# Splitting a block's weights into high and low parts 1024 columns at a time

## The chip, the core and the metric

The kernel runs on one core of one Trainium2 chip. Its time is the device time of one execution in microseconds; lower is better. The engines of a core work side by side: TensorE (PE, matrix products and transposes), VectorE (DVE), ScalarE (ACT), GpSimd (POOL), and SyncE (SP), which here only issues DMA transfers.

## The reference

One decoder layer on 512 tokens of width 1024, in float32. A normalized input is projected by one matrix of 6936 columns; the columns feed two token mixers in parallel. Mixer A is sparse attention with eight heads of 64 in two groups (compressed keys through a small two-layer network per 32 tokens, selected blocks, a window). Mixer B is retention with four heads, in chunks of 128. Gates merge both, and one output projection and a second norm follow.

```python
h = rms_norm(x, norm_pre)
proj = h @ w_in
(q_n, k_c, v_c, k_s, v_s, k_w, v_w, g_n, z_n,
 q_r, k_r, v_r, z_r, m_a, m_b) = jnp.split(proj, split_points(), axis=-1)
...
y_a = (o_a * jax.nn.silu(z_n)) @ w_nsa_o
y_b = (o_b * jax.nn.silu(z_r)) @ w_ret_o
merged = jax.nn.sigmoid(m_a) * y_a + jax.nn.sigmoid(m_b) * y_b
x = x + rms_norm(merged @ w_out, norm_post)
```

## The kernel before

**Two parts for every operand.** Products keep near float32 precision by splitting each operand into a high part (the value rounded to fp32r, a float32 format that TensorE takes) and a low part (value minus high part, also fp32r). A product is then three matmuls: high by high, high by low, low by high. Activations are split where they arise; weights are split as they stream in.

**The weight stream.** All weights lie in one DRAM array in the order of use, in loads of 128 partitions by 1024 columns (560 for block C): two *halves* of 512 (280) columns, each the rows k of one step of 128 of a product's inner dimension. `load_next` (line 323) loads them into a ring of four `raw` tiles. `splitter` takes half after half: `cp_any` rounds it into a `whi` tile (line 197 on ScalarE, or line 205 on VectorE where that engine would be done sooner), and `split_lo` subtracts into a `wlo` tile (line 209 on VectorE, through `sub_split` and `tt`). There are nine `whi` and nine `wlo` tiles of 512 columns (`NW`). A half may be split once the half nine places before it has been used up by its last matmul. Block C has buffers of its own (`WC`).

**Blocks.** The program on TensorE goes block by block: A (512 columns, all four token tiles at once, k by k), C (280 columns), Q, two hidden blocks of the compression network (`hidden`: each half is used by four matmuls of 256 columns and is then free), then by `PLAN` the blocks Z, MA, ZR, QK, VR, ZR, QK, VR, MB, NO, RO, MA, MB, NO, RO, and two output blocks. Most blocks have eight halves and run in four passes (`nat`, `tra`): each pass is one tile of the output and uses all eight halves with three matmuls each, so the halves become free one by one during the last pass. Transposes are matmuls by an identity (line 234); all other matmuls are at line 230. Attention, retention and the tails that evict results are written as further coroutines.

**The order of the work.** The class `Order` runs these coroutines when the program is built. It keeps a clock for TensorE and one for each other engine, advanced by a cost formula per instruction, and issues the coroutine of the lowest priority number that is ready by its clock; `main` with the blocks has the last priority, so that whatever else is ready goes ahead of it. What comes out is a fixed list of instructions for each engine: at run time each engine works through its list in order and waits for what its next instruction needs. A split has priority 0 if its half is at most two ahead (`SOON`) of the one that `main` wants, and 4, after all attention work, otherwise (`rank`). `split_lo` holds back while VectorE's planned backlog exceeds `SLACK`, 700 ns, unless its rank is 0.

Of the kernel before, what the change touches and what calls it, by code (L numbers as in the profile page):

```python
# [11 lines left out]
FR = mybir.dt.float32r  # L12
# [6 lines left out]
P = 128  # L19
SEQ, D = 512, 1024  # L20
NT = SEQ // P
KD = D // P
# [2 lines left out]

C_Q, C_A, C_C, C_Z = 0, 512, 1024, 1304
C_QR, C_KR, C_VR, C_ZR, C_MA, C_MB = 1816, 2328, 2840, 3864, 4888, 5912
NR, NW = 4, 9
PLAN = (("Z", 0), ("MA", 0), ("ZR", 0), ("QK", 0), ("VR", 0), ("ZR", 1), ("QK", 1), ("VR", 1),
        ("MB", 0), ("NO", 0), ("RO", 0), ("MA", 1), ("MB", 1), ("NO", 1), ("RO", 1))  # L30
MAIN = 9
# [114 lines left out]
def block_kernel(ctx: ExitStack, tc, x, xT, g_pre, ws, small, w2s, norm_post, rope_r, dmask, out):  # L146
# [6 lines left out]
    wp = ctx.enter_context(tc.tile_pool(name="wts", bufs=1))  # L153
# [9 lines left out]
    def at(kb, n, dt=FT):  # L163
        o = int(kb * 256)
        return (arena_r if dt == FR else arena_f)[:, o:o + n]
# [6 lines left out]
    od = Order()  # L172
# [27 lines left out]
    def cp_any(o, i, r=0.0):  # L200

        cd = copy_ns(o, i)
        if od.begin("act", r) + act_ns(o, i) <= od.begin("dve", r, near(i)) + cd + DVE_BIAS:
            return act(o, i, r=r)
        V.tensor_copy(o, i)
        return od.op("dve", cd, r, near(i))
# [35 lines left out]
    def sub_split(lo, src, hi, r, e="dve"):  # L242
        return tt(lo, src, f(hi), OP.subtract, r, e)
# [59 lines left out]
        off += P * sum(pieces)  # L303

    raws, parts, done = [], [], []
    WC = [tuple(at(44, 4480, FR)[:, (2 * p + i) * 280:(2 * p + i + 1) * 280] for i in range(2)) for p in range(KD)]

    def in_ring(p):

        return min(p, KD) + max(p - 2 * KD, 0)  # L310
    hook = {}

    def queue(i, j):

        return S if i + j == 0 else DMA

    def load_next():
        i = len(raws)
        if i < len(loads):
            raw = rp.tile([P, 1024], FT, name="raw", tag="raw", bufs=NR)  # L320
            o, c, r = loads[i][0], 0, parts[2 * (i - NR) + 1][2] if i >= NR else 0.0
            for j, n in enumerate(loads[i][1]):
                queue(i, j).dma_start(raw[:, c:c + n], ws[o:o + P * n].rearrange("(p n) -> p n", p=P))
                e = od.dma(P * n * 4, r)
                o, c = o + P * n, c + n
            raws.append((raw, e))
            for fn in hook.get(i, ()):
                fn()
# [5 lines left out]
    nxt = [0]  # L334

    def splitter():
        for i, (_, pieces) in enumerate(loads):
            n = sum(pieces)
            for k in range(2):
                p = 2 * i + k  # L340
                own = KD <= p < 2 * KD
                yield lambda: own or in_ring(p) < in_ring(len(done)) + NW
                while len(raws) <= i:
                    yield lambda: len(raws) > i or len(raws) < NR or len(parts) > 2 * (len(raws) - NR) + 1
                    if len(raws) <= i:
                        load_next()
                r = max(raws[i][1], done[-1] if done and not own else 0.0)
                yield r, "act"
                m = n // 2
                src = raws[i][0][:, k * m:(k + 1) * m]  # L350
                if own:
                    hi, lo = WC[p - KD]
                else:
                    hi = wp.tile([P, 512], FR, name="whi", tag="whi", bufs=NW)
                    lo = wp.tile([P, 512], FR, name="wlo", tag="wlo", bufs=NW)
                vh, vl = hi[:, :m], lo[:, :m]
                e = cp_any(vh, src, r)
                od.spawn(split_lo(p, hi, lo, src, vh, vl, e), rank(p))
                nxt[0] = p + 1
                yield  # L360

    def split_lo(p, hi, lo, src, vh, vl, r):
        yield lambda: rank(p)() == 0 or od.eng["dve"] <= od.now + SLACK
        yield r
        r = sub_split(vl, src, vh, r)
        yield lambda: len(parts) == p
        parts.append((hi, lo, r))
        if p % 2 and len(raws) <= p // 2 + NR:
            load_next()

    used, wanted = [0], [0]
# [1 line left out]
    def rank(p):  # L373

        return lambda: 0 if p <= wanted[0] + SOON else 4
# [911 lines left out]
    od.spawn(h_split(), 0)  # L1287
    od.spawn(norms(), 1)
    od.spawn(splitter(), lambda: rank(nxt[0])())
    od.spawn(edges(), 1)  # L1290
    od.spawn(main(), MAIN)
# [101 lines left out]
```

## Time and profile before

| what | us |
|---|---|
| median of three runs | 531.09 |
| lowest and highest run | 531.02, 531.74 |
| profiled execution, first to last instruction | 529.4 |
| TensorE busy | 519.1 |
| VectorE busy | 390.4 |
| ScalarE busy | 253.4 |

The profiled execution has 7318 instructions; its own time is known by its span alone, which begins at the first and ends at the last instruction. The granted clock of TensorE is at full speed in all 40 slices of the page:

```profile
PEclk9999999999999999999999999999999999999999
```

In the lists below a name such as `bank` or `wlo` is that of a tile; `arena_f` and `arena_r` are two large tiles in which most intermediate results have a place; `nat` are four work tiles. A time "x7" in a row covers seven instructions in a row. Lengths of instructions that follow each other overlap a little, so that the distance from start to start, and not the length, is what an engine needs for one.

### The profile page before, as it was taken

Reading aid. Unit: us, or ns where it says so; the run is one execution under the profiler, and the core shown is the slowest. Engines: PE = TensorE matmul, PEld = TensorE weight load, DVE = VectorE, ACT = ScalarE, POOL = GpSimd, SP = SyncE. Lnnn points to the kernel's source line nnn. Section 1 sums busy time; section 2 is a strip of 40 time slices with the busy share of each in tenths; the row PEclk is TensorE's granted clock in tenths of the full one; section 3 lists DMA queues with packets and bytes.
Section 4 is the critical chain, followed back from the end, with each engine's and each line's share of the span. In section 5 each row is a group of like instructions: output and inputs, shape, how many; then the busy total and the mean of one; then the engine's idle time right before and its main releaser. Section 6 shows DMA issues by size and latency. Waiting matters only on the chain.

```text
span 529.4 us, 7318 instructions
## 1 busy us (share of the span) xinstructions
PE 519.1 (98%) x2636; PEld 437.3 (83%) x2636; DVE 390.4 (74%) x925; ACT 253.4 (48%) x551; POOL 12.6 (2%) x32
## 2 busy tenths in 40 slices
PE   8998999999999999999999999999999999999995
PEld 7896888888888888888888888888888888888885
DVE  6799799989989899998767896777737235345533
ACT  6764588537356494565636253525304224123411
POOL 1000000000000000000010000000000000000000
PEclk9999999999999999999999999999999999999999
DMA  8931127401313013150412342131814043304022
GB/s 327 381 121 54 46 75 251 153 1 42 119 40 109 13 40 120 40 194 5 143 38 80 99 132 67 41 120 40 316 43 158 17 142 121 119 1 158 1 98 101
DMA packets 18131, 55.18 MB, mean 104 GB/s; under 512 B 2096, under 2 KB 3120, under 8 KB 18096
## 3 DMA queue, kind: packets, MB, share of 16 engines
q1 hardware_dynamic: 17808, 54.46, 30.2%
q8 instruction: 20, 0.33, 0.3%
q10 hardware_dynamic: 288, 0.27, 0.2%
q14 instruction: 15, 0.12, 0.1%
HBM read 52.63 MB, written 2.10 MB: 103 GB/s over the span
## 4 chain that ended last, share of the span: by engine, by line
PE 89%; DVE 7%; issue 2%; DMA 1%; ACT 0%; POOLq 0%; DVEq 0%; POOL 0%; ACTq 0%
PE bank L230 83%; PE bank L234 6%; DVE arena_f L209 2%; DVE wlo L209 2%; DVE arena_r L209 1%; DMA raw<-in_stream_dram 1%; DVE arena_f L519 1%; DVE nat L209 0%; DVE arena_f L218 0%; DVE arena_f L798 0%; ACT nat L197 0%; DVE arena_f L222 0%; ACT whi L197 0%; POOLq L1389 0%; POOL rr L209 0%
## 5 line engine op out<-in xcount | busy, mean ns | idle before, releaser
L197 ACT ACTIVATE whi<-raw 128x512 fp32r<-128x512 f32 x150 | 89.8, 627 | 51.2 <-PE bank L230 43.6
L209 DVE TENSOR_TENSOR wlo<-raw,whi 128x512 fp32r<-128x512 f32 x160 | 103.2, 686 | 7.2 <-ACT whi L197 6.5
L230 PE MATMUL bank<-whi,hTh 128*128 128x512 f32 x256 | 98.9, 401 | 0.8 <-ACT whi L197 0.8
L230 PE MATMUL bank<-wlo,hTh 128*128 128x512 f32 x256 | 96.3, 391 | 0.0
L230 PE MATMUL bank<-whi,hTl 128*128 128x512 f32 x256 | 96.2, 391 | 0.0
L230 PE MATMUL bank<-arena_r 128*128 128x256 f32 (+2 forms) x328 | 69.7, 335 | 0.0
L197 ACT ACTIVATE arena_r<-bank 128x512 fp32r<-128x512 f32 (+2 forms) x80 | 44.6, 571 | 47.9 <-PE bank L234 47.7
L230 PE MATMUL bank<-hTh,whi 128*128 128x512 f32 x160 | 63.2, 395 | 0.0
L230 PE MATMUL bank<-hTh,wlo 128*128 128x512 f32 x160 | 62.5, 391 | 0.0
L230 PE MATMUL bank<-hTl,whi 128*128 128x512 f32 x160 | 62.4, 390 | 0.0
L230 PE MATMUL bank<-arena_r,whi 128*128 128x512 f32 x192 | 59.2, 389 | 0.0
L230 PEld LDWEIGHTS bank<-whi,hTl 128*128 128x128 f32 x256 | 48.0, 188 | 10.5
L230 PEld LDWEIGHTS bank<-arena_r 128*128 128x128 f32 x328 | 51.1, 190 | 6.1 <-DVE stat L798 0.2
L230 PEld LDWEIGHTS bank<-whi,hTh 128*128 128x128 f32 x256 | 48.1, 188 | 9.5 <-ACT whi L197 1.0
L230 PEld LDWEIGHTS bank<-wlo,hTh 128*128 128x128 f32 x256 | 48.2, 188 | 9.0 <-DVE wlo L209 0.4
L209 DVE TENSOR_TENSOR arena_r<-bank,arena_r 128x512 fp32r<-128x512 f32 (+2 forms) x72 | 46.5, 656 | 7.4 <-ACT arena_r L197 6.8
L230 PE MATMUL bank<-whi,arena_r 128*128 128x512 f32 (+1 forms) x176 | 48.8, 351 | 0.0
L230 PEld LDWEIGHTS bank<-arena_r,whi 128*128 128x128 f32 x192 | 36.0, 188 | 7.6 <-DVE sg L222 0.2
L234 PE MATMUL bank<-ident,arena_f 128*128 128x128 f32 (+1 forms) x260 | 37.1, 274 | 1.6 <-DVE arena_f L519 1.0
L234 PEld LDWEIGHTS bank<-ident,arena_f 128*128 128x128 f32 (+1 forms) x260 | 30.4, 138 | 8.4 <-DVE arena_f L519 1.5
L230 PE MATMUL bank<-arena_r,wlo 128*128 128x512 f32 x96 | 37.4, 389 | 0.0
L197 ACT ACTIVATE arena_f<-arena_f,stat 128x512 f32<-128x512 f32 (+3 forms) x64 | 35.3, 555 | 3.5 <-DVE stat L798 3.4
(117 smaller groups left out, 670.7 us busy)
## 6 DMA issues: line engine op xcount, KB each, us to landing
raw<-in_stream_dram SPq DMA_DIRECT2D x79, 512.0 KB, 3.9
arena_f<-in_x_dram SPq DMA_DIRECT2D x8, 512.0 KB, 7.1
arena_f<-in_xT_dram SPq DMA_DIRECT2D x8, 256.0 KB, 5.8
arena_f<-in_rope_r_dram SPq DMA_DIRECT2D x8, 256.0 KB, 2.6
out_dram<-arena_f SPq DMA_DIRECT2D x6, 256.0 KB, 2.0
raw<-in_stream_dram SPq DMA_DIRECT2D x4, 280.0 KB, 7.1
arena_f<-in_norm_post_dram SPq DMA_DIRECT2D x1, 512.0 KB, 7.8
out_dram<-arena_f SPq DMA_DIRECT2D x2, 192.0 KB, 1.9
```

The costliest lines, as they stand in the source:

```text
L197: S.activation(o, i, func, **kw)
L209: (V if e == "dve" else G).tensor_tensor(o, a, b, op=op)
L230: T.matmul(ps, a, b, start=start, stop=stop)
L234: T.transpose(ps, a, idn)
L519: V.tensor_copy(kd.rearrange("p (a r c) -> p a r c", a=n, r=2), kn[:, a:b].rearrange("p (a c) -> p a c", c=64).unsqueeze(2).broadcast_to([ ...
```

## The change

From load 4 on (`WHOLE`), that is for all blocks but A, both halves of a load are rounded by one instruction over 1024 columns (560 for C) and subtracted by another. For A's four loads the two halves are split one after the other as before. The `whi` and `wlo` tiles are 1024 columns wide and there are four of each (`NW // 2` with `NW` = 8), so that a pair of halves shares one buffer and the buffer is free when both halves are used up. Both halves of a pair get the rank of the first. The stream, the loads and all matmuls and transposes stay the same in number and size; 160 subtractions of 512 columns become 76 of 1024 and 8 of 512, and 8 of 280 become 4 of 560.

```diff
-NR, NW = 4, 9
+NR, NW, WHOLE = 4, 8, 4
...
-    WC = [tuple(at(44, 4480, FR)[:, (2 * p + i) * 280:(2 * p + i + 1) * 280] for i in range(2)) for p in range(KD)]
+    WC = [tuple(at(44, 4480, FR)[:, (2 * q + i) * 560:(2 * q + i + 1) * 560] for i in range(2)) for q in range(KD // 2)]
...
     def splitter():
         for i, (_, pieces) in enumerate(loads):
             n = sum(pieces)
-            for k in range(2):
-                p = 2 * i + k
-                own = KD <= p < 2 * KD
-                yield lambda: own or in_ring(p) < in_ring(len(done)) + NW
-                while len(raws) <= i:
-                    yield lambda: len(raws) > i or len(raws) < NR or len(parts) > 2 * (len(raws) - NR) + 1
-                    if len(raws) <= i:
-                        load_next()
-                r = max(raws[i][1], done[-1] if done and not own else 0.0)
+            own = KD <= 2 * i < 2 * KD
+            yield lambda: own or in_ring(2 * i) + 2 <= in_ring(len(done)) + NW
+            while len(raws) <= i:
+                yield lambda: len(raws) > i or len(raws) < NR or len(parts) > 2 * (len(raws) - NR) + 1
+                if len(raws) <= i:
+                    load_next()
+            r = max(raws[i][1], done[-1] if done and not own else 0.0)
+            if own:
+                hi, lo = WC[i - KD // 2]
+            else:
+                hi = wp.tile([P, 1024], FR, name="whi", tag="whi", bufs=NW // 2)
+                lo = wp.tile([P, 1024], FR, name="wlo", tag="wlo", bufs=NW // 2)
+            whole = i >= WHOLE
+            for k in range(1 if whole else 2):
                 yield r, "act"
-                m = n // 2
-                src = raws[i][0][:, k * m:(k + 1) * m]
-                if own:
-                    hi, lo = WC[p - KD]
-                else:
-                    hi = wp.tile([P, 512], FR, name="whi", tag="whi", bufs=NW)
-                    lo = wp.tile([P, 512], FR, name="wlo", tag="wlo", bufs=NW)
-                vh, vl = hi[:, :m], lo[:, :m]
+                c = slice(0, n) if whole else slice(k * (n // 2), (k + 1) * (n // 2))
+                src, vh, vl = raws[i][0][:, c], hi[:, c], lo[:, c]
                 e = cp_any(vh, src, r)
-                od.spawn(split_lo(p, hi, lo, src, vh, vl, e), rank(p))
-                nxt[0] = p + 1
+                od.spawn(split_lo(2 * i + k, n // 2, 2 if whole else 1, src, vh, vl, e), rank(2 * i + k))
+                nxt[0] = 2 * i + k + (2 if whole else 1)
                 yield
 
-    def split_lo(p, hi, lo, src, vh, vl, r):
+    def split_lo(p, m, n, src, vh, vl, r):
...
-        parts.append((hi, lo, r))
-        if p % 2 and len(raws) <= p // 2 + NR:
+        for k in range(n):
+            parts.append((vh[:, k * m:(k + 1) * m], vl[:, k * m:(k + 1) * m], r))
+        if len(parts) % 2 == 0 and len(raws) <= p // 2 + NR:
             load_next()
```

Since costs and buffers enter the plan, the lists of TensorE, VectorE, ScalarE and SyncE come out in another order; GpSimd's list stays the same. Three places follow.

*VectorE, tails of blocks A and C.* `nat_100`, `nat_102` hold key tiles, `arena_f<-bank,cst` of 64 partitions adds the position bias to transposed keys and frees a bank, `arena_r<-arena_f,arena_r` of 128x16x64 splits the result. Before:

```order
L209 TENSOR_TENSOR arena_f<-bank_85,cst 64x2x8x16 x4
L209 TENSOR_TENSOR arena_r<-bank_86,arena_r 128x2x128
L209 TENSOR_TENSOR wlo<-raw,whi 128x512
L209 TENSOR_TENSOR arena_f<-nat_102,cst 128x32
L209 TENSOR_TENSOR arena_f<-nat_102,cst 128x2x8 x2
L209 TENSOR_TENSOR nat_102<-arena_f 128x2x16
L209 TENSOR_TENSOR wlo<-raw,whi 128x512
L209 TENSOR_TENSOR arena_f<-bank_86,cst 64x2x8x16 x4
L209 TENSOR_TENSOR wlo<-raw,whi 128x512 x2
```

With the change:

```order
L209 TENSOR_TENSOR arena_r<-bank_85,arena_r 128x2x128
L209 TENSOR_TENSOR wlo<-raw,whi 128x1024
L209 TENSOR_TENSOR arena_r<-bank_86,arena_r 128x2x128
L209 TENSOR_TENSOR arena_f<-nat_102,cst 128x32
L209 TENSOR_TENSOR arena_f<-nat_102,cst 128x2x8 x2
L209 TENSOR_TENSOR nat_102<-arena_f 128x2x16
L209 TENSOR_TENSOR arena_f<-bank_85,cst 64x2x8x16 x4
L209 TENSOR_TENSOR arena_f<-bank_86,cst 64x2x8x16 x4
L209 TENSOR_TENSOR arena_r<-arena_f,arena_r 128x16x64 x2
```

The single subtractions around the position-bias adds have become one pair ahead of them, and the adds of the last two tiles stand together.

*VectorE and TensorE, from the hidden blocks to Z.* VectorE's list with the change, from the last pair of the hidden blocks (the first row) over the gelu of the first hidden block (the rows of 128x128) to Z's four pairs:

```order
L209 TENSOR_TENSOR wlo<-raw,whi 128x1024
L209 TENSOR_TENSOR arena_r<-bank_85,arena_r 128x512
L226 RECIPROCAL stat<-stat 128x1
L218 TENSOR_SCALAR arena_f<-arena_f,stat,gate 128x512
L209 TENSOR_TENSOR wlo<-raw,whi 128x1024 x2
L209 TENSOR_TENSOR arena_f<-bank_86,arena_f 128x128
L209 TENSOR_TENSOR arena_f<-arena_f 128x128
L218 TENSOR_SCALAR arena_f<-arena_f 128x128
L209 TENSOR_TENSOR arena_f<-arena_f 128x128
L209 TENSOR_TENSOR wlo<-raw,whi 128x1024 x2
```

TensorE's list at the start of Z before (`bank_81<-hTh,whi` is Z's first matmul of a half, the others are attention):

```order
L230 MATMUL bank_81<-hTh,whi 128x512
L230 MATMUL bank_81<-hTl,whi 128x512
L230 MATMUL bank_81<-hTh,wlo 128x512
L230 MATMUL bank_83<-arena_r 128x512 x2
L230 MATMUL bank_81<-hTh,whi 128x512
L230 MATMUL bank_81<-hTl,whi 128x512
L230 MATMUL bank_81<-hTh,wlo 128x512
L234 MATMUL bank_86<-ident,arena_f 128x128 x4
L234 MATMUL bank_85<-ident,arena_f 128x128 x4
```

With the change the first seven halves of Z, 21 matmuls, follow each other without other work between them.

*VectorE, from RO 1 to the first output block.* `sg` rows are the tails of RO's last two tiles, `arena_r<-sg` the split of the merged result. Before:

```order
L209 TENSOR_TENSOR wlo<-raw,whi 128x512
L209 TENSOR_TENSOR arena_r<-sg_106,arena_r 128x512
L205 CAST whi<-raw 128x512
L209 TENSOR_TENSOR wlo<-raw,whi 128x512 x5
L222 SCALAR_TENSOR_TENSOR arena_f<-arena_f,bank_82 128x512
L209 TENSOR_TENSOR sg_107<-sg_107,arena_f 128x512
L209 TENSOR_TENSOR wlo<-raw,whi 128x512 x2
L209 TENSOR_TENSOR arena_r<-sg_107,arena_r 128x512
```

With the change:

```order
L209 TENSOR_TENSOR wlo<-raw,whi 128x1024
L209 TENSOR_TENSOR arena_r<-sg_106,arena_r 128x512
L209 TENSOR_TENSOR wlo<-raw,whi 128x1024
L222 SCALAR_TENSOR_TENSOR arena_f<-arena_f,bank_82 128x512
L209 TENSOR_TENSOR sg_107<-sg_107,arena_f 128x512
L209 TENSOR_TENSOR wlo<-raw,whi 128x1024 x2
L209 TENSOR_TENSOR arena_r<-sg_107,arena_r 128x512
```

Six of the eight halves stood ahead of the last tile's tail, now two pairs, four halves.

## The prediction

> **What bounds the kernel now.** I read the page's busy table first, then the engines by stretches, the chain that ended last in order of time, and the single instructions where that chain leaves TensorE.
>
> ```profile
> PE 519.1 (98%) x2636; PEld 437.3 (83%) x2636; DVE 390.4 (74%) x925; ACT 253.4 (48%) x551; POOL 12.6 (2%) x32
> ```
>
> TensorE is busy for 98% of the span, so 80 instructions fewer on VectorE and 75 fewer on ScalarE can shorten only the stretches where TensorE waits. The same engines by stretch (columns: length, then PE, PEld, DVE, ACT, POOL busy with counts, clock, DMA):
>
> ```profile
> 27.30:52.30 25.00, 23.21 (x154) 20.05 (x153) 23.85 (x78) 13.33 (x36) 0.94 (x4) 1.00 0.24 81
> 68.00:85.60 17.60, 17.27 (x110) 14.70 (x108) 16.75 (x44) 15.24 (x32) 0.00 (x0) 1.00 0.44 133
> 92.00:250.00 158.00, 158.00 (x823) 132.97 (x822) 145.21 (x395) 91.47 (x230) 0.00 (x0) 1.00 0.22 74
> 250.00:365.00 115.00, 115.00 (x604) 98.05 (x603) 87.68 (x195) 49.82 (x96) 5.96 (x8) 1.00 0.26 83
> ```
>
> Of these only the first two leave TensorE idle, 25.00 - 23.21 = 1.8 us and 0.3 us; there VectorE is busy 95% of the time. From 92 to 250 us it is 92% busy as well, but TensorE never runs dry. The chain says the same (start, length, what):
>
> ```profile
> 27.27 0.70 ACT nat L197
> ...
> 52.24 0.44 PE bank L234 x2
> ...
> 67.97 0.70 ACT nat L197
> ...
> 85.58 1.23 PE bank L230 x7
> ...
> 365.89 152.55 PE bank L230 x676
> ```
>
> VectorE leads from 27.3 to 52.2 us (tails of blocks A and C) and from 68.0 to 85.6 us (end of Q, the two hidden blocks). Behind that TensorE leads: 152.55/676 = 0.226 us for a matmul, so 0.68 us for the three of one half.
>
> **The change, part by part.** *What one merged instruction costs.* Groups, then single instructions on VectorE:
>
> ```profile
> L209 DVE TENSOR_TENSOR wlo<-raw,whi 128x512 fp32r<-128x512 f32 x160 | 103.2, 686 | 7.2 <-ACT whi L197 6.5
> L197 ACT ACTIVATE arena_f<-arena_f 128x1024 f32<-128x1024 f32 x4 | 4.2, 1062 | 1.8 <-DMA arena_f<-in_x_dram 1.3 <-DVE arena_r L209 0.6
> L197 ACT ACTIVATE whi<-raw 128x512 fp32r<-128x512 f32 x150 | 89.8, 627 | 51.2 <-PE bank L230 43.6 <-DMA raw<-in_stream_dram 5.3 <-ACT whi L197 0.4
> ```
> ```profile
> 52.10 1.22 DVE L209 TENSOR_TENSOR arena_r<-arena_f,arena_r 128x1024 fp32r<-128x1024 f32 x1
> 53.24 0.29 DVE L519 COPY arena_f<-nat 128x256 f32<-128x256 f32 x1
> 372.75 2.49 DVE L209 TENSOR_TENSOR wlo<-raw,whi 128x512 fp32r<-128x512 f32 x4
> ```
>
> The kernel already has a 1024-wide subtraction of the same kind: 1.22 us alone, and the next instruction starts 53.24 - 52.10 = 1.14 us later. Four 512-wide ones in a row take 2.49 us, which is (2.49 - 0.69)/3 = 0.60 us from one to the next. A pair so costs 1.14 in place of 1.20 us: 0.06 us saved, 76 times, 4.6 us of VectorE's 390. On ScalarE the 1024-wide form takes 1.06 us at most (that row also sums its squares) against two of 0.63 us, which overlap a little. All of it lies under TensorE's work except in the two stretches.
>
> [...]
>
> *The ring.* Nine halves become four pairs. A block of eight halves fills them, so nothing of the next block can be split until the last pass over the current one has used up a whole pair. A pair is free 6 halves before it is needed (it was 8 with nine singles), 6 x 0.68 = 4.1 us (5.4). The way from a free buffer to ready weights is 1.06 + 1.22 us and two handovers of up to 0.2 us, 2.7 us, against 0.63 + 0.69 + 0.4 = 1.7 us. The spare time falls from 3.7 to 1.4 us at every block boundary. How far VectorE is behind at such a place shows here, at the boundary before the first output block:
>
> ```profile
> 480.23 0.68 DVE L222 SCALAR_TENSOR_TENSOR arena_f<-arena_f,bank 128x512 f32<-128x512 f32 x1
> ...
> 481.55 1.28 DVE L209 TENSOR_TENSOR wlo<-raw,whi 128x512 fp32r<-128x512 f32 x2
> ```
> ```profile
> 482.35 0.39 PE L230 MATMUL bank<-wlo,arena_r 128*128 128x512 f32 x1
> ```
>
> The first row opens the tail of the last tile of RO 1. The new order puts the pairs for k = 4, 5 and 6, 7 behind the first two instructions of that tail (last place above), so the first of them starts at 481.55 and is ready at 481.55 + 1.14 = 482.69 us; TensorE wants its low part at 482.35 us. Wait: 0.3 us. The other late boundaries have one tail less in the way, or read the low part last: 0 us, bounds 0 to 0.3 us for this term.
>
> *First stretch.* The adds of the position bias have this row:
>
> ```profile
> L209 DVE TENSOR_TENSOR arena_f<-bank,cst 64x256 f32<-64x256 f32 x14 | 8.6, 614 | 0.2
> ```
>
> The new order has two pairs where VectorE had six single subtractions; the second half of the next tiles' keys moves behind them (first place above). VectorE has 6 x 0.60 - 2 x 1.14 = 1.3 us less to do there. But TensorE's transposes are moved too: a transpose needs a bank that four such adds (2.4 us) empty, and laying the rows' lengths end to end in the new order I find TensorE waiting for them four times, 0.3, 0.6, 0.3 and 0.6 us (an estimate), 1.8 us in all against 1.8 us idle now. I take -0.1 us, which is the two merged pairs; bounds -1.3 (all of it reaches TensorE) and +0.5 us (one more of those waits).
>
> *Hidden blocks.* The hidden blocks start at the first row, and block Z starts at the last; between them eight transposes, after four matmuls of the first hidden block:
>
> ```profile
> 75.35 0.28 PE L230 MATMUL bank<-whi,arena_r 128*128 128x256 f32 x1
> ...
> 75.81 1.03 PE L234 MATMUL bank<-ident,arena_f 128*128 128x128 f32 x8
> 76.60 0.36 PE L230 MATMUL bank<-whi,arena_r 128*128 128x256 f32 x1
> ...
> 90.56 0.40 PE L230 MATMUL bank<-hTh,whi 128*128 128x512 f32 x1
> ```
>
> From first to last stand 15.2 us, and by these pitches about 12.9 us of TensorE work (64 matmuls of 256 columns at (75.81 - 75.35)/4 = 0.115 us, 24 transposes at (76.60 - 75.81)/8 = 0.10 us, ten matmuls of 512 columns at 0.226 us, six small ones, an estimate of 0.8 us): 2.3 us of waiting, because TensorE uses a half in four matmuls, 0.46 us, and VectorE makes one in 0.60 us. Eight pairs take 9.1 instead of 9.6 us, and the new order puts more attention work between them. I take -0.5 us, bounds -1.0 and 0.
>
> *Start of Z.* The rows that the new order strings together:
>
> ```profile
> 84.18 0.16 DVE L226 RECIPROCAL stat<-stat 128x1 f32<-128x1 f32 x1
> ...
> 84.84 1.29 DVE L209 TENSOR_TENSOR wlo<-raw,whi 128x512 fp32r<-128x512 f32 x2
> 86.04 0.29 DVE L209 TENSOR_TENSOR arena_f<-bank,arena_f 128x128 f32<-128x128 f32 x1
> ...
> 87.16 1.28 DVE L209 TENSOR_TENSOR wlo<-raw,whi 128x512 fp32r<-128x512 f32 x2
> ```
> ```profile
> 91.25 0.62 PE L230 MATMUL bank<-arena_r 128*128 128x512 f32 x2
> 91.70 0.39 PE L230 MATMUL bank<-hTh,whi 128*128 128x512 f32 x1
> ```
>
> From the last hidden pair to Z's third pair VectorE has: one 512-wide subtraction 0.60, reciprocal and scaling 84.84 - 84.18 = 0.66, two pairs 2.28, the four gelu steps 87.16 - 86.04 = 1.12, a pair 1.14: 5.8 us. TensorE, over the same way, has eight hidden matmuls 0.9, two attention matmuls 91.70 - 91.25 = 0.45, two transposes 0.2, and 14 matmuls of Z without any filler between them 3.2: 4.8 us. It waits 1.0 us if both start level; before, Z's first halves had attention work between them (91.25 is the first) and waited for nothing. Bounds 0 and 1.0; VectorE is the later engine there, so I take 0.7 us.
>
> *Loads.* Each stream load still brings both halves, and the next is issued when its pair is split, as before behind the second half. Their cover is that a raw tile is loaded a block ahead; without it a landing of 3.9 us would show.
>
> ```profile
> raw<-in_stream_dram SPq DMA_DIRECT2D x79, 512.0 KB, 3.9
> ```
>
> *Sum.* -0.1 - 0.5 + 0.7 + 0.3 = +0.4 us on the profiled span of 529.4 us, 529.8 us. The median of the runs, 531.09 us, is 1.7 us above that span (what lies around the instructions); I keep this, and forecast 531.5 us, no change that can be told. About 0.2% (1.06 us) is what a measurement here can tell from none.
>
> **The rivals.** *Faster*: the stretches led by VectorE shorten by all that it saves, and the fillers still suffice at Z: -1.3 - 0.5 = -1.8 us, 529.3 us. For it speaks that VectorE is on the chain for 42 us; against it that the order of TensorE is fixed when the program is written, by costs that let VectorE be earlier than it is, and the waits come from that, not from the subtractions.
>
> *Slower*: the spare 1.4 us at block boundaries is too little while VectorE is 92% busy. From 92 to 365 us there are eight boundaries. Where a pair finds another pair and one other instruction ahead of it, 1.14 + 0.69 = 1.83 us, TensorE waits 1.83 - 1.4 = 0.43 us; eight times is 3.4 us, 534.5 us. It decides once VectorE is more than 1.4 us behind at a boundary and no attention or retention matmul stands in the gap. For it: the row of 92 to 250 us. Against: TensorE has over 800 instructions there, many of them attention work that fills gaps.
>
> *No saving at all*: the 1024-wide forms cost twice the 512-wide ones. The row of 1.22 us speaks against it; it would move the forecast by +0.6 us, to 532.1 us, still no change.
>
> **How the numbers follow.** No change 0.42 (with the last rival in it), own range 530.2 to 532.1 us; faster 0.27; slower 0.31, since of the bounds -1.3, -1.0, 0, 0 and +0.5, 0, +1.0, +0.3 with up to 3.4 us at the boundaries the losses reach farther. The whole range is 529.4 to 534.2 us: it goes to the faster rival's time and nearly to the slower one's, and leaves out about one in five.
>
> **What would show it.** Merged subtractions 1.14 us apart, whi in at most 1.06 us. TensorE idle from 27 to 52 us near 1.8 us again: first stretch right; under 0.8 us: the faster rival. From the end of Q to Z less waiting than 2.3 us, and a wait for wlo of up to 1 us in Z's first tile. A row of TensorE waiting for wlo at 482 us, by 0.3 us. Idle TensorE between 92 and 365 us, where it has none, is the slower rival. I am wrong if the waits between blocks there add up to over 1 us, or if TensorE's idle time in the first stretch halves.

## The result, and the profile after

| kernel | median, us | lowest and highest | profiled span |
|---|---|---|---|
| before, six runs beside after | 531.41 | 531.02, 533.40 | 529.4 |
| after, six runs | 535.17 | 534.22, 536.92 | 532.5 |

The ratio is 1.0062 with a 95% interval of 1.0043 to 1.0081: slower by 3.3 us (the medians stand 3.8 us apart, the profiled spans 3.1 us). The forecast was 531.5 us, no change, range 529.4 to 534.2 us. The runs of most kernels here fall on two levels 1.5 to 2 us apart, so that ratios compare whole sets of runs; in the profiles of e2, e7, e9, e12, e14, e15 and e17 TensorE gets its full clock at 9.5 to 10.8 us, not at 4.5 to 6.0 us as in the others, and loses some 2 us more in the first 27 us, ahead of all that is changed.

What the merged instructions themselves cost came out as forecast. The busy row of the page of after, and two groups with shapes kept apart:

```profile
PE 521.2 (98%) x2636; PEld 436.3 (82%) x2636; DVE 383.5 (72%) x840; ACT 247.1 (46%) x476; POOL 15.4 (3%) x32
...
L209 DVE TENSOR_TENSOR wlo<-raw,whi 128x1024 fp32r<-128x1024 f32 x76 | 91.4, 1219 | 8.1 <-ACT whi L197 7.4
L197 ACT ACTIVATE whi<-raw 128x1024 fp32r<-128x1024 f32 x73 | 77.0, 1058 | 43.1 <-PE bank L230 37.2 <-DMA raw<-in_stream_dram 3.6 <-ACT whi L197 1.1
```

VectorE has 6.9 us less to do (390.4 before; 4.6 us were forecast) and ScalarE 6.3 us less; TensorE's matmuls and transposes are the same 2636, and yet the span is 3.1 us longer.

To see where, I add up from the trace, for each matmul and transpose, by how much the start of the next one comes later than is usual after one of its kind. These are sums over all 2636, in us of waiting by stretch:

| stretch, us | before | after | e1 | e3 | e5 | e6 | e9 | e10 | e13 | e14 |
|---|---|---|---|---|---|---|---|---|---|---|
| 27 to 53, A and C | 3.5 | 4.8 | 3.6 | 3.4 | 3.5 | 4.7 | 4.2 | 4.6 | 3.0 | 2.9 |
| 68 to 100, hidden, Z | 2.4 | 2.4 | 2.1 | 2.7 | 1.2 | 2.4 | 3.7 | 5.1 | 5.6 | 7.2 |
| 100 to 250 | 1.6 | 3.1 | 3.4 | 4.6 | 2.6 | 1.2 | 4.2 | 4.4 | 2.8 | 4.3 |
| 250 to 300 | 0.7 | 1.4 | 0.6 | 1.4 | 6.0 | 4.4 | 1.8 | 1.7 | 1.0 | 1.9 |
| 300 to 365 | 0.8 | 0.9 | 0.9 | 0.9 | 0.8 | 0.8 | 1.6 | 0.8 | 1.3 | 0.8 |

(e1 to e14 are the experiments below; matmuls at a lower clock count as waiting here. What counts as usual is a choice: another one shifts a row as a whole, and differences between kernels by 0.4 us at most.) After loses 1.2 us in the tails of A and C and 2.2 us from 100 to 300 us; the rest nearly cancels.

**Block boundaries.** The waits of weight loads (PEld, TensorE's load of one operand of a matmul) for low parts from 92 to 365 us, first of before, then of after (us in total, times, longest):

```profile
PEld bank L230 <- DVE wlo L209: 0.4, 1, 0.4
```
```profile
PEld bank L230 <- DVE wlo L209: 3.3, 10, 0.5
```

Ten short waits for low parts where there was one. One of the ten lies in a hidden block, at 92.4 us; the other nine lie in the first pass of a block, each at the first half of a pair. They aren't all of the 2.2 us: from 100 to 300 us weight loads wait 4.6 us in after and 0.7 us in before, and 2.9 and 0.4 us of that is for low parts, the rest for other results of VectorE. (A weight load waits longer than the matmuls lose: 0.46 us against 0.2 us in the example.) The example, VectorE's list and then TensorE's:

```profile
263.86 1.02 DVE L209 TENSOR_TENSOR arena_r<-arena_f,arena_r 128x512 fp32r<-128x512 f32 x2
264.79 2.35 DVE L209 TENSOR_TENSOR wlo<-raw,whi 128x1024 fp32r<-128x1024 f32 x2
```
```profile
265.64 0.40 PE L230 MATMUL bank<-whi,hTh 128*128 128x512 f32 x1
266.06 0.50 PE L230 MATMUL bank<-wlo,hTh 128*128 128x512 f32 x1
```

The high part is there at 265.64 us. Its low part is ready when the first of the two pairs ends, at 264.79 + 1.22 = 266.01 us, and the matmul starts at 266.06 us instead of 265.64 + 0.23 = 265.87 us. Nothing else stood in that gap, and two splits of another result stood ahead of the pair.

**The norm row.** ScalarE, then TensorE:

```profile
49.86 1.06 ACT L197 ACTIVATE arena_r<-arena_f 128x1024 fp32r<-128x1024 f32 x1 [5.84 <-DVE arena_f L209]
51.11 1.06 ACT L197 ACTIVATE arena_r<-arena_f 128x1024 fp32r<-128x1024 f32 x1 [0.20 <-DVE arena_f L209]
52.08 0.58 ACT L197 ACTIVATE rsrow<-bank 128x512 f32<-128x512 f32 x1
```
```profile
51.14 0.44 PE L234 MATMUL bank<-ident,arena_f 128*128 128x128 f32 x2 [0.41 <-DVE arena_f L209]
52.71 0.44 PE L234 MATMUL bank<-ident,arena_f 128*128 128x128 f32 x2 [1.14 <-ACT rsrow L197]
```

The transposed norm row sits in a bank that the next key transposes need. It is evicted behind two 1024-wide roundings, which wait for the adds of the position bias; and these adds the new order puts together, all eight behind the pair. TensorE loses 1.3 us. In before the same eviction stood behind the same two roundings, at 51.41 us, but TensorE had fewer keys left by then, and its next transposes, at 52.24 us, came after it.

**Start of Z.** ScalarE, then TensorE:

```profile
94.97 1.06 ACT L197 ACTIVATE whi<-raw 128x1024 fp32r<-128x1024 f32 x1 [0.68 <-DMA raw<-in_stream_dram]
95.93 0.37 ACT L197 ACTIVATE arena_f<-bank 128x256 f32<-128x256 f32 x1
```
```profile
95.39 0.27 PE L230 MATMUL bank<-wlo,arena_r 128*128 128x256 f32 x1
96.35 0.44 PE L234 MATMUL bank<-ident,arena_f 128*128 128x128 f32 x2 [0.69 <-ACT arena_f L197]
```

A rounding waits for its load, the eviction behind it waits for the rounding, and TensorE for the eviction. What the hidden blocks gain is lost here.

### The profile page after: what moved, and what is told of

Read it like the earlier page. It is cut to its first block, busy times and chain, and to the rows that moved or that the text cites. A ratio compares the mean times of both kernels' runs of the same rounds, so it can differ in the third digit from the quotient of the medians.

```text
span 532.5 us, 7125 instructions
## 1 busy us (share of the span) xinstructions
PE 521.2 (98%) x2636; PEld 436.3 (82%) x2636; DVE 383.5 (72%) x840; ACT 247.1 (46%) x476; POOL 15.4 (3%) x32
## 4 chain that ended last, share of the span: by engine, by line
PE 84%; DVE 7%; DMA 4%; issue 2%; ACT 1%; SPq 0%; POOLq 0%; DVEq 0%; POOL 0%; ACTq 0%
PE bank L230 79%; PE bank L234 5%; DMA raw<-in_stream_dram 4%; DVE arena_f L209 2%; DVE wlo L209 2%; DVE arena_r L209 1%; ACT whi L197 1%; DVE arena_f L218 0%; DVE nat L209 0%; DVE arena_f L798 0%; DVE arena_f L519 0%; SPq L436 0%; ACT nat L197 0%; ACT arena_r L197 0%; DVE arena_f L222 0%
## 5 line engine op out<-in xcount | busy, mean ns | idle before, releaser
L209 DVE TENSOR_TENSOR wlo<-raw,whi 128x1024 fp32r<-128x1024 f32 (+1 forms) x84 | 96.8, 1168 | 8.8 <-ACT whi L197 8.1
L197 ACT ACTIVATE whi<-raw 128x1024 fp32r<-128x1024 f32 (+1 forms) x79 | 80.6, 1025 | 44.2 <-PE bank L230 37.2
```

The lines of the kernel that those rows point to most:

```text
L197: S.activation(o, i, func, **kw)
L209: (V if e == "dve" else G).tensor_tensor(o, a, b, op=op)
```

## The experiments

**e1 to e4: ring, width and plan, one at a time.** e1, before with eight single halves:

```diff
-NR, NW = 4, 9
+NR, NW = 4, 8
```

> The kernel before with eight single buffers in place of nine; nothing else. Theory L (the waits at block boundaries from 100 to 300 us, 2.2 us with the change, come from pairs being ready late: free buffer 6 halves ahead, 2.7 us to refill): here a buffer is free 7 halves = 4.8 us ahead and refilled in 1.7 us, 3.1 us to spare, so hardly a wait: 531.4 to 531.9 us. Rival R (they come from the lost ninth half, of which nothing is ready before the last pass): the same waits here, 533.3 us or more. Rival P (any new order of the plan costs or gains that much by chance): no fixed value, 529.5 to 534.

Ratio 1.0021 (1.0002 to 1.0040), which is 532.5 us on the 531.41 of before: between theory L (531.4 to 531.9) and rival R (533.3 or more), with 1.8 us more waiting from 100 to 250 us, near the 2.2 us that R named. It decides neither.

e2, pairs in shared buffers, but every instruction 512 wide:

```diff
-NR, NW, WHOLE = 4, 8, 4
+NR, NW, WHOLE = 4, 8, 999
```

> The changed kernel with pair buffers (four), but every half rounded and subtracted by instructions of 512 columns. L: pair buffers cost 6 instead of 8 halves of notice, but the first half of a pair is ready after 1.7 us: 2.4 us to spare, waits of 0 to 1 us from 100 to 300 us: 531.4 to 532.4 us. R: 2.2 us of waits as with the change, 533.3 us. If the long instructions alone matter (rival W): 531.4 us and no waits.

Ratio 1.0019 (1.0001 to 1.0036), 532.4 us: the upper end of theory L.

e3, wide instructions from block Z on:

```diff
-NR, NW, WHOLE = 4, 8, 4
+NR, NW, WHOLE = 4, 8, 20
```

> The changed kernel, but the 1024-wide instructions only from load 20 on, that is from block Z: C, Q and the hidden blocks are split by halves in pair buffers. L: the 1.3 us wait for rsrow at 51 us goes (it hangs on the order in the tails of A and C), the waits from 100 to 300 us stay: 533.0 to 533.8 us. R: the same. W: the same. If the rsrow wait does not hang on the wide instructions: 534.5 us.

Ratio 1.0064 (1.0044 to 1.0085), 534.8 us: above the 533.8 us of L, R and W. With single halves in the early blocks the wait for the norm row is gone, but from 100 to 300 us there are now 6.0 us of waiting, 1.5 us more than in after, although the splits there follow the same rules. So two plans of one way of splitting differ by as much as the causes that I was looking for.

e4 was to show that directly, with another constant of the planner in before:

```diff
-MARGIN = 50.0
+MARGIN = 48.0
```

> The kernel before with the planner's MARGIN at 48 instead of 50 ns: costs, buffers and instructions unchanged, only the order is drawn anew. L, R and W: within 1 us of the kernel before, 530.5 to 532.4 us, no waits of over 0.1 us for wlo from 100 to 300 us. P: a difference of 2 us or more either way.

Ratio 0.9997 (0.9980 to 1.0015), but the plan hardly moved: the run decides nothing.

**e5 to e8: the same splits, another plan.** `SLACK` of 650 and 750 ns, in before (e5, e6) and in after (e7, e8); it changes 725 to 1007 of the 2636 rows of TensorE's list (by tile and shape, buffer numbers left out).

```diff
-SLACK = 700.0
+SLACK = 650.0
```

> The kernel before, nine single halves, with one planning constant changed: a subtraction whose half is not urgent is held back while VectorE's planned backlog exceeds 650 ns, not 700. Splits, buffers and instructions are those of before; some hundreds of places in TensorE's and VectorE's lists change. Theory M (the loss of 3.8 us belongs to the change itself, to the missing ninth half and the 1024-wide instructions): the time stays within 0.1% of before, and TensorE waits some 2.3 us from 100 to 300 us as before. Theory P (the plan of before is a lucky draw, and every plan drawn anew loses 1 to 3 us, whatever is split how): ratio 1.002 to 1.006, and the waits from 100 to 300 us rise from 2.3 to 3.5 us or more. The fourth run, where the constant hardly moved the plan, could not tell them apart.

> As the run before it, with 750 ns instead of 700: a second plan for nine single halves. Theory M: within 0.1% of before. Theory P: ratio 1.002 to 1.006. If the two plans of nine halves differ by more than 0.2% between themselves, plans scatter by as much as the parts of the loss that the first runs gave (0.2% for the ninth half, 0.4% for the wide instructions), and those parts can't be read from one plan each.

> The changed kernel with the same 650 ns as the first run of this set, to be compared with it: the same redraw for four pairs. Theory M: it stands 0.6% above the first run of this set, as after stands above before. Theory P: the two differ by less than 0.3%, the pairs with a redraw of their own may come out faster than after itself (ratio to before 1.003 to 1.006).

> The changed kernel with 750 ns, to be compared with the second run of this set. Theory M: 0.6% above it; from 27 to 53 us about 4.8 us of waiting with the wait for the transposed norm row behind both 1024-wide roundings, from 100 to 300 us about 4.5 us. Theory P: under 0.3% above it.

| constant | nine singles | four pairs |
|---|---|---|
| 650 | 1.0112 (1.0092 to 1.0133) | 1.0112 (1.0092 to 1.0131) |
| 750 | 1.0071 (1.0051 to 1.0090) | 1.0062 (1.0045 to 1.0078) |

Theory M fails for the time as a whole: before itself, planned anew, is as slow as the pairs. Theory P has the sign, and that pairs and singles differ by less than 0.3%, but 1.0112 and 1.0071 lie above its 1.002 to 1.006. In e5 one wait makes most of it. VectorE's list, then TensorE's:

```profile
262.18 0.43 DVE L209 TENSOR_TENSOR arena_r<-arena_f,arena_r 128x256 fp32r<-128x256 f32 x1
262.64 1.41 DVE L222 SCALAR_TENSOR_TENSOR arena_r<-bank,rs,arena_r 128x512 fp32r<-128x512 f32 x2
```
```profile
259.53 0.57 PE L230 MATMUL bank<-arena_r 128*128 128x256 f32 x4
263.44 0.50 PE L230 MATMUL bank<-whi,hTh 128*128 128x512 f32 x1 [3.35 <-DVE arena_r L222]
```

A block's next tile waits for a bank whose eviction VectorE does late, and TensorE has nothing else. No split is late there. e6 has the same wait (1.9 us) at 263 us.

**e9 and e10: one way of splitting in the other's order.** The turns of all coroutines but the splits are recorded from one plan and replayed in the other kernel; the splits find their places by the planner's rules. TensorE's list is then, row for row, that of before (e9, pairs) or of after (e10, singles), and so are VectorE's and ScalarE's but for the splits.

```diff
-    od = Order()
+    od = Replay()
...
+            turn = SEQUENCE[self.step] if self.step < len(SEQUENCE) else -1
+            mine = [c for c in self.cos if c[4] in (None, turn) or turn < 0]
```

> The splits of the changed kernel (four pairs, 1024-wide) with the turns of all other coroutines replayed as they stood in the plan of before: TensorE's list is that of before, row for row, only the splits find their own places on VectorE and ScalarE. Theory P (what costs is the order drawn anew, not the pairs): as before or up to 0.5 us faster, ratio 0.999 to 1.002. Theory M (pairs that come later and free their buffers later cost by themselves): ratio 1.006 or more. Theory F (an order fits only the splits that it was drawn for; the redraw wins part of the loss back): ratio above 1.010, with waits for wlo at most block boundaries from 100 to 365 us, over 6 us in all.

> The reverse: nine single halves as before, with the turns of all other coroutines replayed as they stood in the plan of the changed kernel; TensorE's list is that of after, row for row. Theory P: as slow as after, ratio 1.005 to 1.008, with the wait for the transposed norm row at 51 us (1.3 us) and the wait before Z's transposes at 95 us still there. Theory M: back at before, ratio 0.999 to 1.002. Theory F: above 1.008, since this order fits nine singles no better than the other order fits pairs.

Ratios 1.0138 (1.0117 to 1.0159) and 1.0140 (1.0116 to 1.0165): theory F's times, both ways. An order fits the splits that it was drawn for, and the redraw had won back more than half of what the pairs cost in the old order. F's detail did not come: it named over 6 us of waits for low parts in e9, and there are 3.2 us in four waits (weight loads, 92 to 365 us):

```profile
PEld bank L230 <- DVE wlo L209: 3.2, 4, 1.6
```

That is nearly the 3.3 us of after, although the order is that of before; and in e10, in the order of after, no weight load waits for a low part in this stretch at all. So these waits go with the way of splitting, and most of the rest of the loss in both runs is waits for other results of VectorE and ScalarE. The boundary at 205 us in before, VectorE's list, then TensorE's:

```profile
201.11 1.29 DVE L209 TENSOR_TENSOR wlo<-raw,whi 128x512 fp32r<-128x512 f32 x2
...
203.89 0.42 DVE L209 TENSOR_TENSOR arena_f<-arena_f,mx 128x256 f32<-128x256 f32 x1
204.24 0.69 DVE L209 TENSOR_TENSOR wlo<-raw,whi 128x512 fp32r<-128x512 f32 x1
```
```profile
204.65 0.39 PE L230 MATMUL bank<-whi,hTh 128*128 128x512 f32 x1
204.98 0.50 PE L230 MATMUL bank<-wlo,hTh 128*128 128x512 f32 x1
```

and the same place in e9:

```profile
207.26 1.22 DVE L209 TENSOR_TENSOR wlo<-raw,whi 128x1024 fp32r<-128x1024 f32 x1
...
209.97 0.43 DVE L209 TENSOR_TENSOR arena_f<-arena_f,mx 128x256 f32<-128x256 f32 x1
210.31 1.22 DVE L209 TENSOR_TENSOR wlo<-raw,whi 128x1024 fp32r<-128x1024 f32 x1
```
```profile
210.03 0.39 PE L230 MATMUL bank<-whi,hTh 128*128 128x512 f32 x1
211.58 0.50 PE L230 MATMUL bank<-wlo,hTh 128*128 128x512 f32 x1 [1.17 <-DVE wlo L209]
```

TensorE reaches the place 210.03 - 204.65 = 5.4 us later than in before, VectorE's first split 6.15 us later. The pair that is needed next so starts 0.7 us late and takes 0.5 us longer than a half: 1.2 us of wait where there was 0.1 us. In e10 the wait for the norm row stands with nine singles as it did with pairs:

```profile
51.98 0.58 ACT L197 ACTIVATE rsrow<-bank 128x512 f32<-128x512 f32 x1
```
```profile
52.61 0.44 PE L234 MATMUL bank<-ident,arena_f 128*128 128x128 f32 x2 [1.14 <-ACT rsrow L197]
```

That wait goes with the order, then, not with the width of the weights' instructions.

**e11 and e12: a third plan of each.**

```diff
-LAG, PE_LAG = 55.0, 60.0
+LAG, PE_LAG = 55.0, 40.0
```

> The kernel before with another planning constant changed: a matmul's data count as ready 40 ns after their engine, not 60. Nine single halves; a third plan for them. Theory P as the two plans with 650 and 750 ns bore it out (1.011 and 1.007): 1.003 to 1.012. Theory L (these two were unlucky, by one wait of 3.4 and 1.9 us near 261 us and the half-speed stretch behind it): 0.999 to 1.003.

> The changed kernel with the same 40 ns, to be set against the run before it. Theory M: 0.6% above it. Theory P: within 0.3% of it on either side. Together with the pairs of runs at 650 ns (1.0112 against 1.0112) and 750 ns (1.0062 against 1.0071) and at 700 and 60 (after, 1.0062 against 1) this makes four plans of each kind.

Singles 1.0001 (0.9985 to 1.0017), pairs 1.0062 (1.0040 to 1.0084): here theory M's difference.

**e13 and e14: what costs in the order of before.** e1's and e2's splits, with the turns of before replayed as in e9.

> Eight single halves instead of nine, all else with the turns of before replayed: TensorE's list is that of before. It splits the loss of the pairs in that order (ratio 1.0138) into the ring and the rest. Theory R (the ninth half is what costs): 1.008 to 1.014. Theory W (the 1024-wide instructions are what costs): 1.000 to 1.003. By thirds (ring, shared buffer, width alike): 1.005.

> Pairs of halves in shared buffers, four of them, but rounded and subtracted one half at a time (512 columns), with the turns of before replayed. Theory R: 1.011 to 1.014 with the buffer that comes free a pair at a time. Theory W: under 1.004, and the step from here to 1.0138 is the width of the instructions.

Eight singles 1.0072 (1.0049 to 1.0096), pair buffers with 512-wide instructions 1.0126 (1.0101 to 1.0151), pairs as in e9 1.0138. e13 stands between the thirds (1.005) and R (1.008 to 1.014), e14 in R's range. With the order of before held, the missing ninth half costs 0.7%, buffers that come free by pairs 0.5%, and the 1024-wide instructions 0.1%, less than the intervals. (In the order of after it is the other way round: there nine singles, e10, are slower than pairs by 0.8%.) Most of it stands in the hidden blocks and Z; TensorE's waits there (68 to 100 us), e13, then e14:

```profile
PE bank L230 <- DVE arena_r L209: 2.5, 2, 1.3
```
```profile
PE bank L230 <- DVE arena_r L209: 4.1, 3, 1.9
```

The waits for low parts alone grow otherwise. Weight loads, 92 to 365 us, e13, then e14:

```profile
PEld bank L230 <- DVE wlo L209: 1.2, 2, 1.0
```
```profile
PEld bank L230 <- DVE wlo L209: 1.7, 2, 1.1
```

From 0.4 us (before) over 1.2 and 1.7 us to the 3.2 us of e9 the wide instruction has the largest step, 1.5 us, though it hardly moves the time.

**e15 and e16: a fourth plan of each.**

```diff
-ISSUE = 8.0
+ISSUE = 4.0
```

> The kernel before with a planning constant changed: 4 instead of 8 ns between instructions of an engine. A fourth redraw for nine halves. Theory P: anywhere from 1.000 to 1.011 like the three others. Theory M: 1.000 to 1.002, the two slow ones being accidents of one wait each.

> The changed kernel with the same 4 ns. Theory M: 0.6% above the run before it. Theory P: within 0.5% of it on either side. If the mean of the five plans of pairs stands less than 0.3% above the mean of the five plans of singles, most of the 0.6% measured belongs to the plan.

Singles 1.0117 (1.0097 to 1.0137), pairs 1.0040 (1.0027 to 1.0054): the pairs are the faster ones, by 0.8%, more than theory P's 0.5% on either side, and against M.

**e17 and e18: plans chosen by their own reckoning.** Both change `LAG` to 50, `PE_LAG` to 40; e17 (singles) `MARGIN` to 55 and `SLACK` to 650, e18 (pairs) `MARGIN` to 45, `SLACK` to 750 and `ISSUE` to 4.

> Nine single halves; the planning constants, of 59 sets tried, whose plan by its own reckoning leaves TensorE waiting least (1.6 us less than the plan of before). Theory A (the plan's own waits rank plans): ratio 0.996 to 0.999, faster than before. Theory B (the chip's waits come from what the plan doesn't know): anywhere from 1.000 to 1.012 like the other redraws of singles.

> The changed kernel, likewise with the set of constants whose plan waits least of 59 (0.6 us more than the plan of before, 4.2 us less than that of after). Theory A: ratio 0.999 to 1.003. Theory B: 1.004 to 1.011 like the five plans of pairs so far. If both come out by theory A, a plan can be chosen before it is run; over the 58 sets tried for both the plans of pairs wait 2.6 us longer in the mean than those of singles, and pairs then are slower beyond the scatter.

Singles 1.0018 (1.0002 to 1.0035), pairs 1.0061 (1.0042 to 1.0079): theory B. The plan's own waits don't pick the fastest plan, and no kernel here beats before.

**Twelve plans together.** Waits of weight loads for low parts from 92 to 365 us, the weight load's wait for the norm row, and the longest wait of TensorE for a result of VectorE other than a low part in those 273 us, each from the views of waits:

| plan | singles: ratio, wlo, norm row, longest | pairs: ratio, wlo, norm row, longest |
|---|---|---|
| as given | 1, 0.4, 0, none | 1.0062, 3.3, 1.4, none |
| SLACK 650 | 1.0112, 0.4, 0, 3.3 | 1.0112, 4.3, 1.4, 1.0 |
| SLACK 750 | 1.0071, 0, 0, 1.9 | 1.0062, 1.2, 0, 0.4 |
| PE_LAG 40 | 1.0001, 0.6, 0, none | 1.0062, 2.6, 1.4, 0.6 |
| ISSUE 4 | 1.0117, 1.8, 0, 1.9 | 1.0040, 3.6, 1.4, none |
| chosen | 1.0018, 0.4, 0, 0.7 | 1.0061, 3.4, 0, 0.4 |

The waits for low parts are 0.6 us in the mean for singles and 3.1 us for pairs, and the wait for the norm row comes in four of six plans of pairs and in none of singles. The first belongs to the splits, as e9 and e10 show; the second to orders that pairs were given more often, since nine singles have it too in the order of after (e10). The times belong to the plans as well: the mean ratio is 1.0053 for singles and 1.0067 for pairs, a difference of 0.0013 before rounding with a standard error of 0.0024 (from the spread of the six, 0.0054 and 0.0024). By what was set down for e16, under 0.3% between the means, most of the 0.6% belongs to the plan; but neither none nor 0.6% is excluded, and whether pairs are slower with the plan averaged out stays open. What the traces show is that after is slower than before for two reasons: it waits more at boundaries and for the norm row, and the plan of before is, with one other, the fastest of six for its own splits. That the constants have these values because they suit nine halves wasn't tested.

## Why the prediction was wrong

**Boundaries: the step that failed.** The part on the ring worked out that the spare time falls from 3.7 to 1.4 us at every boundary from 92 to 365 us, and then the sum gave these boundaries no term. The "slower" rival had the mechanism and 3.4 us for it; measured are 2.2 us more waiting from 100 to 300 us, and of the 3.9 us by which weight loads wait longer there 2.5 us, about two thirds, are for low parts. The rest is for other results of VectorE, which nothing in the prediction named. The reason against the rival, that attention work fills the gaps, came from TensorE's count of instructions and not from the places. The term belonged into the sum. Its origin the prediction had right: with TensorE's order held, the waits for low parts follow the splits (0.4 us before and 3.2 in e9; 3.3 in after and none in e10), and both parts of the shrunken spare time take part, the notice (e13, e14) and the longer way through the wide instructions (e9), by one trace each. The handovers, put at up to 0.2 us each, are 0.03 to 0.10 us in the traces of before and after (0.03 us from a rounding to its subtraction, 0.05 us from a subtraction to the weight load), so the spare time was a little larger than worked out; the loss of 2.3 us stands.

**First stretch: mis-sized.** Forecast -0.1 us with a bound of +0.5, measured +1.2. TensorE idles 25.00 - 22.68 = 2.3 us between 27.3 and 52.3 us, not 1.8; this window ends inside the wait for the norm row, and up to 53.2 us it is 2.7 us:

```profile
27.30:52.30 25.00, 22.68 (x150) 19.20 (x148) 24.20 (x75) 11.60 (x29) 1.89 (x4) 1.00 0.30 99
27.30:53.20 25.90, 23.17 (x153) 19.68 (x152) 25.10 (x75) 12.25 (x31) 1.89 (x4) 1.00 0.29 95
```

The waits for banks behind the position-bias adds are there, four times as forecast, 1.5 us in all where 1.8 us were estimated:

```profile
PE bank L234 <- DVE arena_f L209: 1.5, 4, 0.6
```

The one that was missed goes through ScalarE: I followed VectorE's new list and TensorE's, and not the eviction of the norm row, which stands behind roundings that wait for those adds.

**Hidden blocks and Z.** Forecast -0.5 and +0.7, +0.2 in all; measured 0.0, by another way than the one worked out. Z waits for an eviction behind a rounding that waits for its load, 0.69 us, where a wait for wlo was forecast. Loads had been costed at nothing because a raw tile is loaded a block ahead; at Z's start that cover is not there: ScalarE's roundings wait for their loads three times in a row, 0.75, 0.68 and 0.34 us (at 93.06, 94.97 and 96.64 us). That the two terms cancel, as they nearly did in the sum, is luck. (The work from the hidden blocks to Z adds up to 12.8 us from the prediction's own rows, not 12.9.)

**RO 1 to the first output block.** Forecast 0.3, measured 0: TensorE has no wait there. **Prices of instructions** were right: 1219 ns in the mean for a merged subtraction and 1058 for a rounding, against 1.22 and 1.06 us; two subtractions in a row start 2.35 - 1.22 = 1.13 us apart (264.79 us), against 1.14. That leaves nothing for "no saving at all".

**What no step had**: the plan as a draw. I read the new order at three places and kept before's order everywhere else in mind. Yet it differed throughout, and plans of the same splits lie up to 1.2% apart. A range of -0.3% to +0.6% around the 531.09 us of before was narrower than that.

## What to carry to other kernels

Where a program sets the order by simulated costs, any change draws the whole order anew: measure that scatter first, with constants that change no work, before the gain of an edit is argued in tenths of a per cent. Merging two instructions into one also merges their buffers' release; count the spare time that is left at each refill, and put a term into the sum where it is less than what may stand ahead in the engine's list (here an estimated 1.4 us against a pair and one other instruction, 1.83 us). To find the cause of a small change, replay one kernel's order in the other, and count waits by their releaser over several plans, since the total time mixes them.

## What the runs showed of the hardware

Each trace records when TensorE's granted clock changes. In e5 it is full from 4.95 to 264.37 us, half to 267.78 us and full to 534.02 us. These stretches are 76, 1 and 78 times 3.413 us long. In before the clock is full from 4.73 to 526.97 us, 153 times that, and in after from 5.95 to 531.60 us, 154 times. (In before the clock falls to half at 526.97 us, behind the last matmul; the digits of the page don't show it.)

In e5, e6 and e14 a long wait of TensorE is followed by half speed (stretches of 3.41 us; PE busy is the first number behind the comma, the clock the third from the end). The stretch of the wait and the next, e5, e6, e14:

```profile
260.95:264.37 3.42, 0.93 (x4) 0.80 (x5) 3.33 (x6) 1.28 (x3) 0.00 (x0) 1.00 0.89 276
264.37:267.78 3.41, 3.41 (x10) 2.48 (x9) 0.54 (x3) 0.42 (x1) 0.00 (x0) 0.50 0.18 60
```
```profile
260.87:264.28 3.41, 1.49 (x9) 1.16 (x9) 3.35 (x6) 2.19 (x5) 0.00 (x0) 1.00 0.77 273
264.28:267.70 3.42, 3.42 (x10) 2.65 (x9) 1.88 (x5) 0.42 (x1) 0.00 (x0) 0.50 0.56 175
```
```profile
91.48:94.90 3.42, 1.52 (x11) 1.23 (x10) 2.26 (x7) 3.21 (x8) 0.00 (x0) 1.00 0.82 275
94.90:98.31 3.41, 3.41 (x11) 2.73 (x10) 2.30 (x7) 1.60 (x4) 0.00 (x0) 0.50 0.54 167
```

TensorE is idle for 73%, 56% and 56% of the first stretch, and the clock of the second is 0.50. In e5 seven matmuls in the slow stretch start 0.43 us apart (from 264.55 to 264.98 us) instead of 0.23 (from 264.01 to 264.24 us), 1.4 us more on top of the wait of 3.35 us. e6 and e14 waited 1.9 us. e15 waits as long, 1.9 us near 246 us, and its clock stays at 1.00; two stretches of 3.41 us share this wait, idle for 24% and 39%:

```profile
242.31:245.73 3.42, 2.60 (x12) 1.83 (x10) 3.42 (x8) 0.69 (x1) 0.00 (x0) 1.00 1.03 303
245.73:249.14 3.41, 2.08 (x9) 1.61 (x10) 3.41 (x14) 1.61 (x8) 0.00 (x0) 1.00 0.54 188
249.14:252.55 3.41, 3.41 (x19) 2.82 (x18) 3.17 (x15) 2.00 (x8) 0.00 (x0) 1.00 0.12 46
```

In after TensorE is idle for 48% of the stretch from 524.78 to 528.19 us, and the clock is at 1.00 in the next, up to 531.60 us. So a wait of 1.9 us was followed by half speed in e6 and e14 and not in e15; what decides it was not shown.
